# Two feature blocks of each feed-forward in plain form, and its entry's arithmetic on VectorE

## The chip, the cores and the metric

The kernel runs on one core of a Trainium2 chip. A core has five engines with queues of their own: TensorE (PE; its weight loads are PEld), VectorE (DVE), ScalarE (ACT), GpSimd (POOL) and SyncE (SP), which here only starts DMA transfers. An engine works through its queue in order; semaphores make one wait for another. The metric is the time of one execution on the device, in microseconds.

## What is computed

Two decoder layers over 1024 tokens of 1024 features, float32. Layer A mixes by causal attention with a forget gate, layer B by dilated attention in three groups over a shared K/V; each is followed by a norm and a gated feed-forward with a short convolution over the tokens:

```python
def conv_ffn(h, w_up, conv_w, conv_b, w_down):
    u = h @ w_up                        # 1024 -> 2 x 2816
    u = causal_depthwise_conv(u, conv_w, width=3) + conv_b
    a, gate = jnp.split(u, 2, axis=-1)
    return (jax.nn.silu(gate) * a) @ w_down

for layer in (A, B):
    x = x + mixer(rms_norm(x, mix_norm_g)) @ w_out
    x = x + conv_ffn(rms_norm(x, ffn_norm_g), ...)
out = rms_norm(x, final_norm_g)
```

## The kernel before, in words

Activations lie with features on partitions. Every float32 operand of a product is split into a high and a low part (`split`, line 149: ScalarE casts, VectorE subtracts), and a product is three matmuls: high-high, high-low, low-high. The activations that feed a projection are `yh` and `yl`, 8 blocks of 128 features by 1024 tokens. Half the tokens are 512 columns: one matmul, one PSUM bank, and one VectorE instruction of 128x512.

`after_mixer` (line 1053) runs the entry of a feed-forward. `first_half` normalises the first half of the tokens (`norm_half`): sums of squares to TensorE (line 183), the root on small tiles, four transposes (line 196), a copy by ScalarE (line 198); then 8 multiplications, four on VectorE (line 213), four on GpSimd (line 230), whose gains ScalarE has multiplied in beforehand (line 206), and 8 splits. Meanwhile TensorE runs the output projection of the second half (`out_proj`, eight tiles, each added into `xT` by VectorE, line 627). Two PSUM banks serve it, so a tile waits for the addition of the last but one.

The up-projection takes a block of 128 features and its gates at once as a 2 x 2 product in seven products instead of eight (Winograd's form of Strassen's). A are the weights, by halves of the inputs; B the normalised activations: B11 and B21 are the first half of the tokens, B12 and B22 the second. Its operands are sums: S1 to S4 of weights (GpSimd, lines 755 and 757) and T1 to T4 of activations. T1 = B12 - B11, T3 = B22 - B12, T2 = T3 + B11, T4 = B21 - B11 - T3. Only two of seven products per block (A11 B11, A12 B21) need the first half alone. `second_half` normalises the second half and makes T1 to T4, partly on GpSimd (lines 681, 682, 694); B11 and B21 - B11 wait in the tiles of the low parts of T2 and T4, where SP stores them (line 660).

`ffn` lists steps, each with a load, a preparation (sums of weights), a split and a use, issued 6, 5, 3 and 0 steps ahead. The first two feature blocks' steps alternate. Step 1 may only be issued behind the second norm's sums on TensorE, steps 2 and 3 behind its transposes. Weight tiles `wh`, `wl` are rings of six, the raw ones `wraw` of three, `fraw` of two. `tap` (line 713) is the convolution, `middle` the gated value `mh`, `ml`, from which the down-projection (`down_step`) starts as soon as two blocks are there. The final order on every engine is set by the framework's scheduler, which plans with a timeline of its own.

At the exit of layer A's feed-forward `norm_half` runs again for each half, without gains.

Of the kernel before, what the change touches and what calls it, by code (L numbers as in the profile page):

```python
# [50 lines left out]
def trunk(ctx, tc, x, a_w_in, a_b_f, a_w_out, b_w_q, b_w_out, kv_norm_g, w_kv,  # L51
# [25 lines left out]
    # activations that feed the projections: high and low parts, features on partitions  # L77
# [45 lines left out]
    def stream(tasks):  # L123
        """tasks: (load, body); each load is issued one task ahead"""
# [11 lines left out]
    def weave(main, filler, ratio, ready=lambda: True):  # L136
        """ratio columns of filler per column of main, once ready; the filler stops at a None"""
# [30 lines left out]
    def square_sums(fp, xT, hf, ds):  # L168
        """sums over the blocks ds of the squares of half the tokens; also 2 KB of free memory"""
        acc, free = halves(fp.tile([P, S], F32, name="ca" if hf else "cg"))  # L170
# [29 lines left out]

    def gained(y, xT, gain, ds, sl):
        """y = xT * gain, or where that is xT itself"""
        if gain is None:
            return [xT[:, d, sl] for d in ds]
        for i, d in enumerate(ds):
            nc.scalar.activation(y[i], xT[:, d, sl], AF.Identity, scale=gain[:, d:d + 1])
        return y
# [55 lines left out]
    def softmax(t, sc_cuts, masks, nm, l, rl):  # L263
        """t = exp(min(s) - s) / sum, for negated scores s = sc + mask; nm: min(s), l: the sum"""
# [12 lines left out]
    def add_parts(dst, po, tmp, view=lambda t: t):  # L277
        """dst = (value high part) p + (value low part) p, rows 0..63 and 64..127 of po"""
# [68 lines left out]
    def project_v_a(vs, hf, w):  # L347
        """values of two pairs for half the tokens: [token, (block, head, high|low of 64)]"""
# [9 lines left out]
    def scores_a(ap, psc, head, qg):  # L358
        """probabilities of query blocks 2qg, 2qg+1"""
# [56 lines left out]
    # ---------------------------------------------------------------- mixer B  # L416
# [3 lines left out]
    def by_residue(g, hf):  # L420
        """tokens of half hf, residue by residue: views of the source and of the result"""
# [8 lines left out]
    def in_order(g, t, m):  # L430
        """places in token order of columns m*512.. of the residue order"""
# [50 lines left out]
    def scores_b(ap, psc, p, g, j, head, nm, ls, m):  # L482
        """probabilities of half m of the query blocks (in residue order), by (key, query) block"""
# [106 lines left out]
    # ---------------------------------------------------------------- after a mixer  # L590
# [113 lines left out]
    def ffn(l, xT, fp, psu, y3, B, norm):  # L704
# [174 lines left out]
        for i in range(-LOAD, n):  # L879
            if i == 0:  # L880
                first, second = norm()
# [349 lines left out]
```

## Time and profile before

| | before |
|---|---|
| time, median of 3 runs (lowest to highest) | 2719.21 us (2717.98 to 2719.22) |
| span of the profiled execution | 2719.0 us |
| TensorE busy | 2606.2 us (96%), 12937 matmuls |
| VectorE busy | 2049.2 us (75%) |
| ScalarE busy | 1402.8 us (52%) |
| GpSimd busy | 757.3 us (28%) |

The page names no other time for the profiled execution than its span. TensorE's busy time includes matmuls that run into each other, so idle time is read from stretches and from the waits, not from the sum. Layer A's feed-forward has its entry from about 600 to 730 us and its exit at 1325 to 1375, layer B's entry is from about 1970 to 2090.

### The profile page before, as it was taken

Reading aid. Unit: us, or ns where it says so; the run is one execution under the profiler, and the core shown is the slowest. Engines: PE = TensorE matmul, PEld = TensorE weight load, DVE = VectorE, ACT = ScalarE, POOL = GpSimd, SP = SyncE. Lnnn points to the kernel's source line nnn. Section 1 sums busy time; section 2 is a strip of 40 time slices with the busy share of each in tenths; the row PEclk is TensorE's granted clock in tenths of the full one; section 3 lists DMA queues with packets and bytes.
Section 4 is the critical chain, followed back from the end, with each engine's and each line's share of the span. In section 5 each row is a group of like instructions: output and inputs, shape, how many; then the busy total and the mean of one; then the engine's idle time right before and its main releaser. Section 6 shows DMA issues by size and latency. Waiting matters only on the chain. (4 is left out here: it accounts for less than half of the span.)

```text
span 2719.0 us, 38066 instructions
## 1 busy us (share of the span) xinstructions
PE 2606.2 (96%) x12937; PEld 2172.9 (80%) x12937; DVE 2049.2 (75%) x4021; ACT 1402.8 (52%) x2937; POOL 757.3 (28%) x904
## 2 busy tenths in 40 slices
PE   7999999997999999999899999999878999999998
PEld 5899988786788888888688888888657888888887
DVE  5677777768976777778777777777799766777786
ACT  6565665654534344444545566566655443444444
POOL 0222222315212211112243454544353122111121
PEclk8999999999999999999999999999878999999999
DMA  5211211522111111111411111113211111112113
GB/s 178 66 55 51 64 56 59 190 82 83 46 49 54 49 52 54 59 51 46 142 36 37 47 40 40 47 40 100 94 63 47 53 49 54 48 55 59 51 47 113
DMA packets 258619, 176.99 MB, mean 65 GB/s; under 512 B 12528, under 2 KB 240504, under 8 KB 258424
## 3 DMA queue, kind: packets, MB, share of 16 engines
q1 hardware_dynamic: 258424, 174.56, 21.1%
q8 instruction: 102, 1.67, 0.3%
q14 instruction: 93, 0.76, 0.1%
HBM read 146.63 MB, written 23.68 MB: 63 GB/s over the span
## 5 line engine op out<-in xcount | busy, mean ns | idle before, releaser
L114 PE MATMUL mm<-yh,wh 128*128 128x512 f32 (+1 forms) x1008 | 402.7, 400 | 18.3 <-DVE xT L627 6.5
L115 PE MATMUL mm<-yl,wh 128*128 128x512 f32 (+1 forms) x1008 | 401.1, 398 | 0.4 <-DMA yl<-o_sp 0.4
L116 PE MATMUL mm<-yh,wl 128*128 128x512 f32 (+1 forms) x1008 | 400.7, 398 | 0.0
L150 ACT CAST wh<-wraw 128x512 fp32r<-128x512 f32 x230 | 142.1, 619 | 365.6 <-PE up L771 322.4
L771 PE MATMUL up<-yl,wh 128*128 128x512 f32 x704 | 278.3, 396 | 17.7 <-DVE yl L151 17.7
L856 DVE TENSOR_TENSOR xT<-mm,xT 128x512 f32<-128x512 f32 x320 | 217.3, 683 | 101.0 <-PE mm L116 99.5
L151 DVE TENSOR_TENSOR wl<-wraw,wh 128x512 fp32r<-128x512 f32 x230 | 168.3, 736 | 152.3 <-ACT wh L150 152.0
L771 PE MATMUL up<-yh,wh 128*128 128x512 f32 x704 | 276.4, 395 | 6.8 <-ACT yh L150 5.8
L771 PE MATMUL up<-yh,wl 128*128 128x512 f32 x704 | 272.6, 394 | 0.0
L114 PEld LDWEIGHTS mm<-yh,wh 128*128 128x128 f32 (+1 forms) x1008 | 190.0, 189 | 58.2 <-issue 10.6
L115 PE MATMUL mm<-ml,wh 128*128 128x512 f32 x576 | 225.3, 391 | 0.5 <-DVE ml L151 0.5
L116 PE MATMUL mm<-mh,wl 128*128 128x512 f32 x576 | 224.3, 389 | 0.0
L114 PE MATMUL mm<-mh,wh 128*128 128x512 f32 x576 | 224.2, 390 | 0.0
L271 ACT ACTIVATE t<-t,nm 128x128 f32<-128x128 f32 (+4 forms) x320 | 185.2, 580 | 73.0 <-DVE nm L266 69.0
L115 PEld LDWEIGHTS mm<-yl,wh 128*128 128x128 f32 (+1 forms) x1008 | 189.9, 188 | 36.9 <-DVE yl L151 1.0
L116 PEld LDWEIGHTS mm<-yh,wl 128*128 128x128 f32 (+1 forms) x1008 | 189.7, 188 | 37.0 <-issue 0.3
L150 ACT CAST pt<-tp 128x128 fp32r<-128x128 f32 (+2 forms) x408 | 150.2, 382 | 111.1 <-PE tp L244 66.2
L755 POOL TENSOR_TENSOR sraw<-fraw 128x512 f32<-128x512 f32 x42 | 68.2, 1623 | 479.2 <-DMA fraw<-in_ffn_w_up_dram 338.2
L151 DVE TENSOR_TENSOR pt<-tp,pt 128x128 fp32r<-128x128 f32 (+2 forms) x408 | 170.8, 430 | 36.3 <-ACT pt L150 33.5
L257 PE MATMUL po<-pt,v 128*128 128x256 f32 x1040 | 192.8, 292 | 3.4 <-DVE og L280 1.1
L93 DVE TENSOR_TENSOR wl<-wraw,wh 128x512 fp32r<-128x512 f32 (+1 forms) x185 | 138.6, 753 | 60.2 <-ACT wh L92 58.0
L771 PEld LDWEIGHTS up<-yl,wh 128*128 128x128 f32 x704 | 134.1, 190 | 48.5 <-DVE yl L151 20.4
(320 smaller groups left out, 6421.1 us busy)
## 6 DMA issues: line engine op xcount, KB each, us to landing
wraw<-in_ffn_w_down_dram SPq DMA_DIRECT2D x104, 256.0 KB
fraw<-in_ffn_w_up_dram SPq DMA_DIRECT2D x84, 256.0 KB
wraw<-in_ffn_w_up_dram SPq DMA_DIRECT2D x84, 256.0 KB
wraw<-in_a_w_in_dram SPq DMA_DIRECT2D x64, 256.0 KB
wraw<-in_w_kv_dram SPq DMA_DIRECT2D x48, 256.0 KB
wraw<-in_a_w_out_dram SPq DMA_DIRECT2D x32, 256.0 KB
xT<-x_sp SPq DMA_DIRECT2D x32, 256.0 KB
wraw<-in_b_w_q_dram SPq DMA_DIRECT2D x24, 256.0 KB
```

Of the source, the lines that this page charges most:

```text
L93: nc.vector.tensor_tensor(out=wl, in0=raw, in1=wh.bitcast(F32), op=ALU.subtract)
L114: nc.tensor.matmul(ps, ah, bh, start=(i == 0), stop=False)
L115: nc.tensor.matmul(ps, ah, bl, start=False, stop=False)
L116: nc.tensor.matmul(ps, al, bh, start=False, stop=(i == n - 1))
L150: nc.scalar.copy(h, src)
L151: return nc.vector.tensor_tensor(out=l, in0=src, in1=h.bitcast(F32), op=ALU.subtract).ins
L257: nc.tensor.matmul(po[:, col:col + 2 * P], v(kb), pt[:, hl, i * 2 * P:(i + 1) * 2 * P], start=(first and i == 0 and hl == 0), stop=(last a ...
L271: nc.scalar.activation(t[:, :n], t[:, :n], AF.Exp, bias=nm[len(sc_cuts) - 1], scale=-1.0, accum_out=l)
L755: nc.gpsimd.tensor_tensor(out=raw[n], in0=raw[a], in1=raw[b], op=op)
L771: nc.tensor.matmul(ps[bank], a[:, c], b[:, k], start=(start and k == 0 and i == 0), stop=(k == KH - 1 and i == 2), skip_group_check=True)
L856: nc.vector.tensor_tensor(out=xT[:, d, sl], in0=ps, in1=xT[:, d, sl], op=ALU.add)
```

## The change

- Blocks 0 and 1 of both feed-forwards are computed in plain form, with eight products each (`plain`, `PLAIN = 2`). First come all products of both blocks with the first half of the tokens (A11 B11, A12 B21, and the same for the gates' rows A21, A22), then those of the second half, where A B12 is accumulated as A B11 + A T1 in the bank that still holds A B11. Their convolutions and gated values (`rest`) come behind.
- The multiplications of the norms and the sums T1 to T4 are all on VectorE; `gained` (ScalarE's multiplication by gains ahead of GpSimd's) is gone.
- `second_half` is cut in two by a `yield`: first T1 and B22, later T2, T3 and T4. The tiles of T3 hold the weights of block 0 until its last product, that of T2's high part holds the sums of squares.

```diff
     def norm_half(fp, psum, xT, gain, hf, raw):
         sl = half(hf)
-        xg = gained(raw[KH:], xT, gain, range(KH, KD), sl)
         r, _ = feature_rstd(fp, psum, xT, hf)
-        for k in range(KH):
-            normed(raw[k], xT, gain, k, sl, r)
-        for k in range(KH):
-            nc.gpsimd.tensor_tensor(out=raw[KH + k], in0=xg[k], in1=r, op=ALU.mult)
         for d in range(KD):
+            normed(raw[d], xT, gain, d, sl, r)
             split(yh[:, d, sl], yl[:, d, sl], raw[d])
...
     def second_half(fp, psum, y3, xT, gain, B, raw, sums):
...
         for k in range(KH):
             normed(b12[k], xT, gain, k, sl, r)
-        for k in range(KH):
             t1 = half_tile(fp)
             nc.vector.tensor_tensor(out=t1, in0=b12[k], in1=b11[:, k], op=ALU.subtract)
             part("T1", k, t1)
+        for k in range(KH):
+            normed(b22[k], xT, gain, KH + k, sl, r)
+            part("B22", k, b22[k])
+        yield steps
...
         for k in range(KH):
-            with tc.issue_after(done) if k else nullcontext():
-                nc.gpsimd.tensor_tensor(out=b22[k], in0=b22[k], in1=r, op=ALU.mult)
-            done = nc.gpsimd.tensor_tensor(out=t3[k], in0=b22[k], in1=b12[k],
-                                           op=ALU.subtract).ins
-        for k in range(KH):
+            nc.vector.tensor_tensor(out=t3[k], in0=b22[k], in1=b12[k], op=ALU.subtract)
             t2 = half_tile(fp)
             nc.vector.tensor_tensor(out=t2, in0=t3[k], in1=b11[:, k], op=ALU.add)
-            last = part("T2", k, t2)
+            part("T2", k, t2)
...
     def up(f):
...
+            def plain(row, hf):
+                a, b, bank, c = row + "1", row + "2", "X" + row, "ca" if row == "A1" else "cg"
+                if hf:
+                    return [lambda: product(a, "T1", bank, False),
+                            lambda: (product(b, "B22", bank, False), snap(c, 1, bank))]
+                return [lambda: product(a, "B11", bank, True),
+                        lambda: (product(b, "B21", "Q", True), snap(c, 0, "Q"),
+                                 add(c, 0, bank, c, 0))]
...
-        first = [up_steps(f) for f in range(2)]
-        steps = [first[f][i] for i0, i1 in ((0, 2), (2, 3), (3, 4), (4, 5), (5, 6), (6, 7))
-                 for f in range(2) for i in range(i0, i1)]
-        done = 2
+        steps, tails = [], []
+        for f in range(PLAIN):
+            now, then, prep, part, rest = up(f)
+            steps += [(ld, lambda n=n, prep=prep: prep(n), lambda n=n, part=part: part(n), use)
+                      for ld, n, use in now]
+            tails.append((then, rest))
+        for then, _ in tails:
+            steps += [(lambda: None,) * 3 + (use,) for use in then]
+        sums_at = len(steps) - 4
+        rests = {len(steps) - 1 + 3 * f: rest for f, (_, rest) in enumerate(tails)}
```

Over the whole kernel TensorE has 48 matmuls more, VectorE 32 instructions more, ScalarE 28 fewer and GpSimd 64 fewer. TensorE's order is the same outside the entries and a place or two at layer A's exit. Three places show what moved; `mm` are banks of the out-projection and the second norm, `up` those of the up-projection.

TensorE in layer A at the sums of squares of the second half (L183); before, the product ahead of it is A11 B11 of block 0 (`up_7794`):

```order
L771 MATMUL up_7794<-yh_80,wh_7658 128x512
L771 MATMUL up_7794<-yl_81,wh_7658 128x512
L771 MATMUL up_7794<-yh_80,wl_7659 128x512
L183 MATMUL mm_7692<-ones_74,ca_7334 128x1 x4
L771 MATMUL up_7813<-yh_80,wh_7662 128x512
L771 MATMUL up_7813<-yl_81,wh_7662 128x512
```

The same place now, where `mm_7620` is the last tile of the out-projection:

```order
L114 MATMUL mm_7620<-yh_80,wh_7587 128x512
L115 MATMUL mm_7620<-yl_81,wh_7587 128x512
L116 MATMUL mm_7620<-yh_80,wl_7588 128x512
L183 MATMUL mm_7670<-ones_74,T2h_7326 128x1 x4
L765 MATMUL up_7747<-yh_80,T3h_7650 128x512
L765 MATMUL up_7747<-yl_81,T3h_7650 128x512
```

A11 B11 of block 0 now stands one tile earlier, and the sums follow the last tile directly.

VectorE in layer A behind the second norm's root, before; `u` become T1, `sraw` are sums of weights:

```order
L213 SCALAR_TENSOR_TENSOR mh_7252<-xT_6410,gains_988,ca_7334 128x512 x2
L213 SCALAR_TENSOR_TENSOR ml_7253<-xT_6410,gains_988,ca_7334 128x512 x2
L676 TENSOR_TENSOR u_7716<-mh_7252,T2l_7244 128x512
L676 TENSOR_TENSOR u_7720<-mh_7252,T2l_7244 128x512
L676 TENSOR_TENSOR u_7724<-ml_7253,T2l_7244 128x512
L151 TENSOR_TENSOR wl_7852<-sraw_7853,wh_7851 128x512
```

And now, where `mh_7250` and `ml_7251` become B22:

```order
L780 TENSOR_TENSOR ca_7760<-up_7728,ca_7760 128x512
L205 SCALAR_TENSOR_TENSOR mh_7248<-xT_6410,gains_988,T2h_7326 128x512 x2
L205 SCALAR_TENSOR_TENSOR ml_7249<-xT_6410,gains_988,T2h_7326 128x512 x2
L205 SCALAR_TENSOR_TENSOR mh_7250<-xT_6410,gains_988,T2h_7326 128x512 x2
L205 SCALAR_TENSOR_TENSOR ml_7251<-xT_6410,gains_988,T2h_7326 128x512 x2
L673 TENSOR_TENSOR u_7691<-mh_7248,T2l_7243 128x512
L673 TENSOR_TENSOR u_7696<-mh_7248,T2l_7243 128x512
L673 TENSOR_TENSOR u_7701<-ml_7249,T2l_7243 128x512
L673 TENSOR_TENSOR u_7706<-ml_7249,T2l_7243 128x512
L151 TENSOR_TENSOR yl_81<-mh_7250,yh_80 128x512 x2
```

All eight multiplications are on VectorE now and stand together; the splits of weight sums are gone from between them.

TensorE in layer B behind the sums of both halves, before; `up_20473` and `up_20515` are A11 B11 of blocks 0 and 1, `up_20492` is A12 B21 of block 0:

```order
L183 MATMUL up_20083<-ones_74,cg_20084 128x1 x4
L183 MATMUL mm_20371<-ones_74,ca_20157 128x1 x4
L196 MATMUL up_20115<-ident_69,nr_20107 128x128 x4
L196 MATMUL mm_20385<-ident_69,nr_20377 128x128 x4
L771 MATMUL up_20473<-yh_80,wh_20337 128x512
L771 MATMUL up_20492<-yh_80,wh_20341 128x512
L771 MATMUL up_20473<-yl_81,wh_20337 128x512
```

And now, with products of four rows of weights of block 0 and the first two of block 1 (`up_20455`, `up_20468`):

```order
L183 MATMUL up_20051<-ones_74,cg_20052 128x1 x4
L183 MATMUL mm_20325<-ones_74,T2h_20125 128x1 x4
L196 MATMUL up_20083<-ident_69,nr_20075 128x128 x4
L765 MATMUL up_20383<-yh_80,T3h_20305 128x512
L765 MATMUL up_20402<-yh_80,T3h_20305 128x512
L196 MATMUL mm_20339<-ident_69,nr_20331 128x128 x4
L765 MATMUL up_20422<-yh_80,T3h_20305 128x512
L765 MATMUL up_20437<-yh_80,T3h_20305 128x512
L765 MATMUL up_20455<-yh_80,wh_20321 128x512
L765 MATMUL up_20468<-yh_80,wh_20379 128x512
L765 MATMUL up_20383<-yl_81,T3h_20305 128x512
```

Two matmuls moved ahead of the second transposes, and six products of the first half are begun before the first low part (`yl`) is needed.

## Rows read from the trace of the kernel before

**Rows 1.** Stretches: length, then busy us (instructions) of PE PEld DVE ACT POOL, clock, DMA.

```profile
850.00:875.00 25.00, 25.00 (x111) 20.55 (x110) 20.11 (x31) 11.66 (x19) 3.97 (x3) 1.00 0.15 43
655.00:722.00 67.00, 54.49 (x223) 42.30 (x222) 64.85 (x77) 35.09 (x62) 33.55 (x21) 0.92 0.11 32
1345.00:1361.00 16.00, 4.23 (x16) 3.31 (x17) 15.76 (x16) 8.16 (x14) 11.68 (x8) 0.66 0.32 99
1987.00:2080.00 93.00, 68.48 (x248) 51.52 (x247) 87.43 (x100) 47.24 (x82) 52.26 (x32) 0.80 0.16 53
```

**Rows 2.** TensorE's waits, longest in total first: us in total, times, longest.

```profile
PE up L771 <- DVE yl L151: 17.7, 6, 5.9
PE mm L114 <- DVE xT L627: 6.5, 3, 3.5
```

**Rows 3.** Timeline of TensorE, layer A's entry: start us, us, [idle before, what ended it].

```profile
631.65 0.47 PE L114 MATMUL mm<-yh,wh 128*128 128x512 f32 x1 [2.71 <-DVE xT L627]
...
640.84 0.77 PE L114 MATMUL mm<-yh,wh 128*128 128x512 f32 x1 [3.51 <-DVE xT L627]
...
655.89 0.95 PE L183 MATMUL mm<-ones,ca 128*128 128x1 f32 x8
...
674.24 0.79 PE L771 MATMUL up<-yl,wh 128*128 128x512 f32 x1 [5.92 <-DVE yl L151]
...
721.74 0.39 PE L114 MATMUL mm<-mh,wh 128*128 128x512 f32 x1
...
725.31 0.61 PE L771 MATMUL up<-T3h,wh 128*128 128x512 f32 x1 [1.41 <-ACT ca L783]
```

**Rows 4.** Timeline of VectorE, layer A's entry.

```profile
619.82 3.59 DVE L213 SCALAR_TENSOR_TENSOR mh<-xT,gains,cg 128x512 f32<-128x512 f32 x2
...
627.35 1.88 DVE L151 TENSOR_TENSOR yl<-mh,yh 128x512 fp32r<-128x512 f32 x3
629.15 1.75 DVE L151 TENSOR_TENSOR yl<-ml,yh 128x512 fp32r<-128x512 f32 x1
...
661.34 3.61 DVE L213 SCALAR_TENSOR_TENSOR mh<-xT,gains,ca 128x512 f32<-128x512 f32 x2 [0.43 <-ACT ca L198]
```

**Rows 5.** Timeline of GpSimd, layer A's entry.

```profile
619.87 3.00 POOL L230 TENSOR_TENSOR mh<-mh,cg 128x512 f32<-128x512 f32 x2 [18.20 <-ACT cg L198]
...
628.71 1.65 POOL L657 TENSOR_TENSOR mh<-mh 128x512 f32<-128x512 f32 x1 [2.43 <-DVE yl L151]
...
636.21 3.33 POOL L657 TENSOR_TENSOR ml<-ml 128x512 f32<-128x512 f32 x2 [0.63 <-DVE yl L151]
```

**Rows 6.** Timeline of VectorE inside layer A's feed-forward, GpSimd idle.

```profile
859.93 1.41 DVE L721 SCALAR_TENSOR_TENSOR u<-cg,conv,u 128x510 f32<-128x510 f32 x2
```

**Rows 7.** Timeline of TensorE, layer B's entry.

```profile
1987.88 0.95 PE L183 MATMUL up<-ones,cg 128*128 128x1 f32 x8
1990.27 1.05 PE L183 MATMUL mm<-ones,ca 128*128 128x1 f32 x8 [1.44 <-DVE ca L175]
...
2079.34 0.39 PE L114 MATMUL mm<-mh,wh 128*128 128x512 f32 x1
...
2083.78 0.56 PE L771 MATMUL up<-T3h,wh 128*128 128x512 f32 x1 [2.43 <-ACT ca L783]
```

**Rows 8.** Timeline of VectorE, layer B's entry.

```profile
1993.69 3.53 DVE L213 SCALAR_TENSOR_TENSOR mh<-xT,gains,cg 128x512 f32<-128x512 f32 x2 [0.78 <-ACT cg L198]
```

**Rows 9.** A stretch of layer B's out-projection; columns as in rows 1.

```profile
1970.50:1990.30 19.80, 18.04 (x84) 14.70 (x82) 16.74 (x27) 13.25 (x24) 1.30 (x1) 1.00 0.23 67
```

**Rows 10.** Timeline of VectorE, exit of layer A.

```profile
1351.25 5.47 DVE L211 TENSOR_TENSOR T3h<-xT,cg 128x512 f32<-128x512 f32 x4
1356.65 1.75 DVE L175 TENSOR_TENSOR ca<-ca,u 128x512 f32<-128x512 f32 x1
```

**Rows 11.** Timeline of TensorE, exit of layer A.

```profile
1358.45 1.86 PE L183 MATMUL up<-ones,ca 128*128 128x1 f32 x8 [5.03 <-DVE ca L175]
```

More of the change, by code (lines that the diff above doesn't have):

```diff
@@ L631, in out_proj, with side @@
                        for d in range(KD)])
+    PLAIN = 2
+    def side(y3, part):
+        return y3.tile([P, KH, H2], F32R, name=part)
     def sides(y3):
@@ L647, in sides @@
                for n, k, t in (("B11", lo, t0), ("T1", lo, t1), ("B21", hi, t0), ("B22", hi, t1))}
-        for n in ("T2", "T3", "T4"):
-            res[n] = tuple(y3.tile([P, KH, H2], F32R, name=n + p) for p in "hl")
+        for n in ("T2", "T4"):
+            res[n] = (None, side(y3, n + "l"))
         return res
@@ L656, in first_half @@
         for k in range(KH):
-            nc.gpsimd.tensor_tensor(out=raw[KH + k], in0=raw[KH + k], in1=raw[k],
+            nc.vector.tensor_tensor(out=raw[KH + k], in0=raw[KH + k], in1=raw[k],
                                     op=ALU.subtract)
@@ L660, in first_half, with second_half @@
                 nc.sync.dma_start(B[n][1][:, k].bitcast(F32), src)
-    def second_half(fp, psum, xT, gain, B, raw, sums):
+    def second_half(fp, psum, y3, xT, gain, B, raw, sums):
         sl = half(1)
         b11, diff = (B[n][1].bitcast(F32) for n in ("T2", "T4"))
-        b12, b22 = raw[:KH], gained(raw[KH:], xT, gain, range(KH, KD), sl)
+        b12, b22 = raw[:KH], raw[KH:]
         r, steps = feature_rstd(fp, psum, xT, 1, sums)
@@ L677, in second_half @@
             part("T1", k, t1)
+        for k in range(KH):
+            normed(b22[k], xT, gain, KH + k, sl, r)
+            part("B22", k, b22[k])
+        yield steps
+        B["T2"] = (side(y3, "T2h"), B["T2"][1])
+        B["T3"] = (side(y3, "T3h"), side(y3, "T3l"))
+        B["T4"] = (side(y3, "T4h"), B["T4"][1])
         t3 = b12
         for k in range(KH):
-            with tc.issue_after(done) if k else nullcontext():
-                nc.gpsimd.tensor_tensor(out=b22[k], in0=b22[k], in1=r, op=ALU.mult)
-            done = nc.gpsimd.tensor_tensor(out=t3[k], in0=b22[k], in1=b12[k],
-                                           op=ALU.subtract).ins
-        for k in range(KH):
+            nc.vector.tensor_tensor(out=t3[k], in0=b22[k], in1=b12[k], op=ALU.subtract)
             t2 = half_tile(fp)
             nc.vector.tensor_tensor(out=t2, in0=t3[k], in1=b11[:, k], op=ALU.add)
-            last = part("T2", k, t2)
-        with tc.issue_after(last):
-            for k in range(KH):
-                part("T3", k, t3[k])
-        with tc.issue_after(done):
-            for k in range(KH):
-                t4 = half_tile(fp)
-                nc.gpsimd.tensor_tensor(out=t4, in0=diff[:, k], in1=t3[k], op=ALU.subtract)
-                with tc.issue_after(last):
-                    part("T4", k, t4)
-        with tc.issue_after(last):
-            for k in range(KH):
-                part("B22", k, b22[k])
-        return steps
+            part("T2", k, t2)
+        for k in range(KH):
+            part("T3", k, t3[k])
+        for k in range(KH):
+            t4 = half_tile(fp)
+            nc.vector.tensor_tensor(out=t4, in0=diff[:, k], in1=t3[k], op=ALU.subtract)
+            part("T4", k, t4)
+        yield None
     LOAD, PREP, SPLIT = 6, 5, 3
@@ L731, in up @@
             raw, w, t, ps = {}, {}, {}, {}
-            pairs = {}
             def load(*names):
@@ L736, in load @@
                     block, half_ = n[1], int(n[2]) - 1
-                    if f != 1:
-                        raw[n] = (wp.tile([P, H2], F32, name="wraw", bufs=3) if block == "1" else
-                                  fp.tile([P, H2], F32, name="fraw", bufs=2))
-                    else:
-                        if block not in pairs:
-                            pairs[block] = mid_tile(fp, "mh" if block == "1" else "ml")
-                        raw[n] = halves(pairs[block].bitcast(F32))[half_]
+                    raw[n] = (wp.tile([P, H2], F32, name="wraw", bufs=3) if block == "1" else
+                              fp.tile([P, H2], F32, name="fraw", bufs=2))
                     fb = f if block == "1" else NF + f
@@ L748, in prep @@
             def prep(n):
-                w[n] = hl()
+                if f == 0:
+                    if not w:
+                        both = side(y3, "T3h"), side(y3, "T3l")
+                        w.update({m: [t[:, i] for t in both]
+                                  for i, m in enumerate(("A11", "A12", "A21", "A22"))})
+                else:
+                    w[n] = hl()
                 a, b, op = {"S1": ("A21", "A22", ALU.add), "S2": ("S1", "A11", ALU.subtract),
@@ L752, in prep @@
                 if a:
-                    raw[n] = (raw["S1"] if n == "S2" and f < 2 else
-                              fp.tile([P, H2], F32, name="sraw", bufs=2))
+                    raw[n] = fp.tile([P, H2], F32, name="sraw", bufs=2)
                     nc.gpsimd.tensor_tensor(out=raw[n], in0=raw[a], in1=raw[b], op=op)
@@ L806, in c11, with rest @@
                 add("ca", 0, "Q", "cg", 0)
-            none = lambda: None
+            def plain(row, hf):
[6 more added lines that the diff above has]
+                                 add(c, 0, bank, c, 0))]
+            def rest():
+                for hf in range(2):
+                    gate(hf)
+                    middle(hf)
+            none = lambda: None
+            if f < PLAIN:
+                first, second = ([use for row in ("A1", "A2") for use in plain(row, hf)]
+                                 for hf in range(2))
+                return [(lambda n=n: load(n), n, use)
+                        for n, use in zip(("A11", "A12", "A21", "A22"), first)], second, prep, part, rest
             return [
@@ L812, in up @@
                 (lambda: load("A12"), "A12",
-                 lambda: (product("A12", "B21", "Q", True), f != 1 and c11())),
+                 lambda: (product("A12", "B21", "Q", True), c11())),
                 (lambda: load("A21", "A22"), "S1",
-                 lambda: (product("S1", "T1", "Z", True), f == 1 and c11())),
+                 lambda: product("S1", "T1", "Z", True)),
                 (none, "S2",
@@ L880, in ffn @@
             if i == 0:
-                first, second = norm()
+                norm = norm()
+                first, second = next(norm)
+            if i == sums_at:
+                next(norm)
             if 0 <= i + SPLIT < n:
@@ L1068, in after_mixer @@
         first_half(fp, up, xT, g_ffn[l], B, raw)
-        sums = square_sums(fp, xT, 1, blocks_done(out_proj(w_out, 1, xT)))
+        sums = square_sums(fp, xT, 1, blocks_done(out_proj(w_out, 1, xT)),
+                           y3.tile([P, S], F32, name="T2h"))
         for hf in ffn(l, xT, fp, psu, y3, B,
-                      lambda: second_half(fp, mm, xT, g_ffn[l], B, raw, sums)):
+                      lambda: second_half(fp, mm, y3, xT, g_ffn[l], B, raw, sums)):
             yield hf, fp, up if hf else mm, y3
```

13 lines of the change are left out of this document (5 added, 8 removed).

## The prediction

> **What bounds the kernel now.** I read the busy shares of stretches first. Inside a feed-forward TensorE is never idle: 111 matmuls in 25 us, 0.226 us each [rows 1]. At the two entries it is not. From 655 to 722 us it gets through 223 matmuls in 67 us, from 1987 to 2080 through 248 in 93 us, at mean granted clocks of 0.92 and 0.80, so part of that time runs at 1.2 GHz instead of 2.4, and VectorE is busy 65 of 67 and 87 of 93 us [rows 1]. The list of TensorE's waits names the culprit: VectorE's low parts of the normalised activations (17.7 us) and its additions into xT (6.5 us) [rows 2]. So the entries are bound by VectorE, the rest by TensorE's columns. The end of every entry is easy to see on TensorE: the first matmul on `mh`, when the first product of the down projection starts, at 721.74 us in layer A [rows 3] and at 2079.34 us in layer B [rows 7]. I forecast when these two points come now; behind them the order of TensorE is nearly the same again.
>
> Why VectorE is slow there is in its own rows. Two multiplications of the norm take 3.59 us while GpSimd runs two of its own [rows 4, 5]. A little later three splits take 1.88 us with GpSimd silent, and the next one 1.75 us alone, under GpSimd's subtraction at 628.71 [rows 4, 5]. So a VectorE instruction of 128x512 costs 0.60 us of the queue by itself ((1.88 - 0.68)/2; 0.67 for the form with a scalar, from two in 1.41 us [rows 6]) and about 1.7 beside GpSimd. Moving GpSimd's work here takes 0.60 to 0.67 us per step and gives back about 1.1 for each VectorE instruction that was held up.
>
> A rule bears on this. The Trainium skill, "SBUF — State Buffer", section "Who interferes with whom", says that a VectorE instruction with two SBUF inputs and a GpSimd instruction that reads SBUF exclude each other for a whole instruction. The rows show a delay of 1.1 us, less than GpSimd's 1.65 us; by the rule each sum that stays on GpSimd at an entry (about four, for feature block 2) would cost VectorE 1.65 instead of 1.1, some 2 us more per entry, which only matters where VectorE is late (second rival).
>
> **The change, part by part.** *Plain form.* Blocks 0 and 1 take 8 products of 12 matmuls instead of 7: 24 matmuls more per layer, 24 x 0.226 = 5.4 us each time, paid in full once TensorE no longer waits. In exchange 8 products (96 matmuls, 21.7 us) need only the first half of the tokens, where 4 did before, and the other 8 need T1 and B22 only; T2, T3 and T4 are first needed by block 2.
>
> *Layer A, out-projection.* Before, TensorE idles 2.71 and 3.51 us for xT [rows 3], whose additions stand behind the norm in VectorE's queue. That norm starts at 619.82 in both kernels. Now 8 multiplications (8 x 0.67 = 5.4), a weight split and four splits of yl (5 x 0.60 = 3.0) stand ahead of the addition: 628.2, and 0.68 plus hand-over gives 629.0 for TensorE instead of 631.65. The second wait goes: that addition stands 7 instructions (4.2 us) later, while a tile takes TensorE 5.4. Three tiles and the first product (84 matmuls, 19.0 us) end at 648.0. But this product now stands ahead of the last tile, so the sums of squares follow that tile directly and nothing covers addition, square and sum. Layer B shows this gap, from the first sums at 1987.88 to the second at 1990.27: 2.4 us [rows 7]. So the sums run at 650.4 instead of 655.89 [rows 3].
>
> *Layer A, second norm.* Its first multiplication came 5.45 us behind the sums (661.34 [rows 4]); now 655.9. VectorE has one addition, 8 multiplications, 4 differences and 13 others (splits, T3, one addition) up to the last split of T1: 18 x 0.60 + 8 x 0.67 = 16.2, hence 672.1. TensorE meanwhile has 12 + 72 matmuls of the first half and 10 more: 650.4 + 0.9 + 0.4 + 94 x 0.226 = 672.9. So it meets T1 ready, 0.8 us ahead, and runs through: 228 matmuls from sums to `mh`, 51.5 us, so **703.2 instead of 721.74: -18.5 us**, the 24 additional matmuls included. (Before it stops in the middle, for instance 5.92 us until 674.24 [rows 3].) T2 and T4 follow on VectorE in 18 instructions (11 us behind T1), T3's low parts 8 later, while TensorE has 96 matmuls (21.7 us) of plain products to cover them.
>
> *Layer B.* Here both sums come together and no out-projection covers the norm; TensorE waits from 1990 on in any case. The weights of blocks 0 to 2 are now split earlier, 8 splits (4.8 us) more in the out-projection, where VectorE is idle 3.1 of 19.8 us [rows 9]; I take 1.0 us of delay, between 0 and 4.8. The first multiplication moves from 1993.69 [rows 8] to 1994.7. Eight of them and a small step: 2000.3, when TensorE gets past its transposes with four high-part matmuls in hand; the first yl is there at 2001.0. From 2000.5, with 0.4 for transposes and 10 matmuls at half clock (10 x 0.2 = 2.0 us; one shows 0.61 busy there, as against 0.39 [rows 3]), it has 94 matmuls of the first half: 2024.1. VectorE: 46 instructions from 1994.7 (16 x 0.67 + 30 x 0.60 = 28.7) end at 2023.4, again just ahead. Then 144 more: 2024.1 + 32.5 = **2056.6 instead of 2079.34: -22.7 us.**
>
> *Exit of layer A.* Four multiplications take 5.47 us beside GpSimd's, the sum behind them 1.75 [rows 10]; eight alone take 4.8 and the sum ends at 1356.7 instead of 1358.4, so the sums on TensorE (1358.45 [rows 11]) move up by 1.5. The first split is no longer last: **-1.5 us**. The norm of the second half has no waiting TensorE; nothing there.
>
> *What costs nothing.* ScalarE loses 16 multiplications by gains and 12 splits; it was not full. On SP the stores of differences now follow VectorE's, done near 636.5, earlier than GpSimd's (639.5 [rows 5]), so the weight loads behind them are not later. Block 2's S1 gets its weight tile only when block 1's first weight is used up (six tiles in the ring), some 687 us; TensorE needs it at 698. T3's tile holds block 0's weights until its products end, about when VectorE arrives there. Each has 0 to 1 us of stall in it; I take 0.
>
> *Behind `mh`.* Before, TensorE waits once more for ScalarE's copy of a bank, 1.41 and 2.43 us [rows 3, 7], both times with half clock behind. That wait stands in the new order too; I leave it. Its bounds: all of it goes, or VectorE's queue is late there.
>
> Sum: -18.5 - 22.7 - 1.5 = -42.7. The profiled execution spans 2719.0 us and the page gives no other time for it; the median of the three runs is 2719.21, so the span stands for the time: **2676 us.**
>
> **The rivals.** *The wait moves behind the plain products.* From T1 to the last low part of block 1's result VectorE has 55 instructions: at 0.62 us they end at 706.2 and 2057.5, TensorE needs them at 707.5 and 2060.9 (19 matmuls behind `mh`). The slack is only 1.3 and 3.4 us. At the pace of the entries before (65/77 = 0.84 and 87/100 = 0.87 [rows 1]) they take 12.2 and 14.0 us longer, so TensorE waits 10.9 and 10.6: 2698 us. For it: the conv taps, block 2's sums on GpSimd and the weights meet there. Against: GpSimd has four steps there, not twenty.
>
> *VectorE stays slow for reasons of its own; slower than before.* Then its queue is the path throughout: 81 instructions in A for the 51.6 us from 655.9 to 707.5, 101 in B for the 66.2 from 1994.7 to 2060.9. The gains of A's out-projection (5.5) and the exit (1.5) go, which leaves 35.7 to lose; it decides from a mean of (51.6 + 66.2 + 35.7)/182 = 0.84 us. At the exit's pace, 15.76/16 = 0.985 [rows 1], the result is 182 x 0.985 - 153.5 = 26 us slower: 2745. Against it: the splits at 0.60 us in the same stretch [rows 4].
>
> *It also cures the tail.* Both bank waits and nine half-clock matmuls (0.2 each) behind either go: 1.41 + 2.43 + 3.6 = 7.4, thus 2669 us.
>
> That the change does not do what it says is excluded by the order: six products of the first half stand behind the norm's transposes.
>
> **How the numbers follow.** Forecast 0.62, wait behind the products 0.18, tail cured 0.13, slow VectorE 0.04, and 0.03 for mixtures that end near the old time. A measurement of this kernel can tell 0.2% from no change, 5 us. Faster 0.93, same 0.03, slower 0.04. The open terms (B's delay 0 to 4.8, the half clock, small stalls) make the forecast 2668 to 2686; the range must reach into the tail's cure below and the moved wait above: 2660 to 2699 us.
>
> **What would show it.** Right: additions in the out-projection within 1 us; GpSimd silent between first norm and block 2; norm multiplications of 0.67 us; TensorE without a gap from the second transposes to `mh`, some 52 us (A). Wrong: VectorE at over 0.7 us in that stretch; TensorE waiting for T1 or B22; new gaps over 5 us at the first matmuls on `mh`; waits for weights.

## The result and the profile after

The changed kernel takes 2685.69 us (median of four runs, 2681.52 to 2687.63) against 2719.21: ratio 0.987, 95% interval 0.9855 to 0.9884. The forecast was 2676, its range 2660 to 2699. The profiled execution took 2685.47 us, of which the program spans 2683.6; the span is 35.4 us shorter than before, where 42.7 were forecast. TensorE is now busy 2602.9 us (12985 matmuls), VectorE 2004.3, ScalarE 1386.8, GpSimd 655.6.

The stretches that answer to [rows 1] (length, then busy us and instructions of PE, PEld, DVE, ACT, POOL, then TensorE's granted clock, DMA share, GB/s): in layer A TensorE is now busy throughout from 655 us to `mh`; in layer B it has 243 matmuls in 61 us instead of 248 in 93. GpSimd has two instructions in each where it had 21 and 32.

```profile
655.00:709.00 54.00, 54.00 (x232) 44.36 (x233) 47.95 (x79) 30.77 (x53) 3.35 (x2) 0.97 0.06 20
...
1987.00:2048.00 61.00, 58.53 (x243) 47.39 (x244) 59.59 (x94) 34.70 (x59) 3.06 (x2) 0.92 0.15 52
```

TensorE's waits (us in total, times, longest): both leaders of [rows 2] are gone, and a new one heads the list, the sums of squares waiting for VectorE.

```profile
PE mm L183 <- DVE T2h L175: 7.7, 2, 4.2
```

This wait in layer A, on the timelines of TensorE, VectorE and GpSimd (start, us, instruction, idle before and what ended it; columns as in [rows 3]):

```profile
649.17 0.39 PE L116 MATMUL mm<-yh,wl 128*128 128x512 f32 x1
653.10 1.87 PE L183 MATMUL mm<-ones,T2h 128*128 128x1 f32 x8 [3.54 <-DVE T2h L175]
654.83 0.78 PE L765 MATMUL up<-yh,T3h 128*128 128x512 f32 x1
...
709.16 0.39 PE L114 MATMUL mm<-mh,wh 128*128 128x512 f32 x1
...
711.97 0.50 PE L765 MATMUL up<-T3h,wh 128*128 128x512 f32 x1 [1.04 <-ACT ca L777]
```

```profile
651.30 1.75 DVE L175 TENSOR_TENSOR T2h<-T2h,u 128x512 f32<-128x512 f32 x1
...
660.88 1.40 DVE L205 SCALAR_TENSOR_TENSOR mh<-xT,gains,T2h 128x512 f32<-128x512 f32 x2
```

```profile
649.56 1.27 POOL L749 TENSOR_TENSOR sraw<-fraw 128x512 f32<-128x512 f32 x1 [59.65 <-DMA fraw<-in_ffn_w_up_dram]
650.91 1.59 POOL L749 TENSOR_TENSOR sraw<-sraw,wraw 128x512 f32<-128x512 f32 x1
652.58 1.60 POOL L751 TENSOR_TENSOR wraw<-wraw,sraw 128x512 f32<-128x512 f32 x1
```

The out-projection's last matmul starts at 649.17, then TensorE waits 3.54 us; the sums run at 653.10 (before 655.89, [rows 3]). The addition behind the last square (651.30) takes 1.75 us, since GpSimd makes block 2's weight sums at the same moment. The sums then take 1.73 us to the next matmul instead of 0.81 (655.89 to 656.70 before), and the matmuls up to about 658.4 come every 0.43 us. A view of that stretch (columns as in [rows 1]) shows a granted clock of 0.50, that is 1.2 instead of 2.4 GHz:

```profile
653.10:658.40 5.30, 5.30 (x17) 4.53 (x18) 0.83 (x5) 0.21 (x1) 1.08 (x1) 0.50 0.00 0
```

`mh` starts at 709.16 instead of 721.74.

Layer B, TensorE and VectorE: the second sums come 5.18 us behind the first (2.39 before, [rows 7]), again with slow additions; VectorE's first multiplication comes 3.48 us behind the second sums, as before (3.42, [rows 7, 8]). `mh` starts at 2048.42 instead of 2079.34.

```profile
1976.80 1.02 PE L183 MATMUL up<-ones,cg 128*128 128x1 f32 x8 [0.81 <-DVE cg L175]
1981.98 1.87 PE L183 MATMUL mm<-ones,T2h 128*128 128x1 f32 x8 [4.15 <-DVE T2h L175]
...
2048.42 0.39 PE L114 MATMUL mm<-mh,wh 128*128 128x512 f32 x1
```

```profile
1978.51 1.74 DVE L175 TENSOR_TENSOR T2h<-T2h,u 128x512 f32<-128x512 f32 x1
...
1980.36 1.56 DVE L175 TENSOR_TENSOR T2h<-T2h,u 128x512 f32<-128x512 f32 x1
...
1985.46 1.41 DVE L205 SCALAR_TENSOR_TENSOR mh<-xT,gains,cg 128x512 f32<-128x512 f32 x2 [0.57 <-ACT cg L198]
```

Where the time went, in sections of TensorE's timeline, us (start: to the last row of `po` matmuls of layer A's attention; A: to the first matmul on `mh`; tail A: to the first sums at the exit; exit: to its last transposes; attention: to layer B's last row of `po` matmuls; B: to first `mh`; tail B: to the end):

| kernel | start | A | tail A | exit | attention | B | tail B | span |
|---|---|---|---|---|---|---|---|---|
| before | 594.6 | 127.2 | 615.0 | 30.6 | 579.1 | 132.9 | 639.7 | 2719.0 |
| after | 596.0 | 113.2 | 613.5 | 31.1 | 580.4 | 114.2 | 635.1 | 2683.6 |
| e1_vec_only | 591.2 | 115.3 | 617.3 | 29.9 | 578.9 | 125.8 | 640.3 | 2698.8 |
| e2_plain_gp | 594.1 | 121.2 | 611.8 | 30.1 | 580.1 | 124.9 | 635.8 | 2698.0 |
| e3_sums_vec | 596.1 | 110.9 | 612.2 | 30.1 | 579.5 | 108.4 | 636.0 | 2673.2 |
| e4_cover | 596.4 | 107.3 | 613.7 | 30.2 | 577.1 | 111.5 | 636.5 | 2672.5 |
| e5_both | 593.2 | 106.8 | 612.1 | 30.0 | 579.9 | 110.7 | 636.2 | 2668.9 |
| e6_plain1 | 596.1 | 113.4 | 620.3 | 30.3 | 582.7 | 116.8 | 640.6 | 2700.3 |
| e7_exit_gp | 595.8 | 113.7 | 613.6 | 31.2 | 583.7 | 111.8 | 636.4 | 2686.2 |
| e8_load | 593.9 | 113.7 | 616.4 | 30.0 | 582.8 | 114.2 | 637.0 | 2688.0 |

So the change is +1.4 us (start), -14.0 (A), -1.5 (tail A), +0.6 (exit), +1.3 (attention), -18.7 (B), -4.5 (tail B). The start ends between 591.2 and 596.4 us in the ten kernels, though the order up to there is the same in all, on every engine; so spans scatter by some us for reasons ahead of the edits, and the sections tell more than the totals. They scatter too: the attention has the same order on every engine in the changed kernel, e4_cover and e8_load, and takes 580.4, 577.1 and 582.8 us.

### The profile page after: what moved, and what is told of

The parts are those of the page before. It is cut to its first block, busy times and chain, and to the rows that moved or that the text cites. A ratio compares the mean times of both kernels' runs of the same rounds, so it can differ in the third digit from the quotient of the medians.

```text
span 2683.6 us, 38044 instructions
## 1 busy us (share of the span) xinstructions
PE 2602.9 (97%) x12985; PEld 2178.6 (81%) x12985; DVE 2004.3 (75%) x4053; ACT 1386.8 (52%) x2909; POOL 655.6 (24%) x840
## 4 chain that ended last, share of the span: by engine, by line
PE 86%; DVE 7%; ACT 3%; issue 2%; DMA 1%; POOL 1%; POOLq 0%; ACTq 0%; SPq 0%; DVEq 0%
PE up L765 30%; PE mm L114 13%; PE mm L115 13%; PE mm L116 13%; PE po L245 4%; PE tp L232 3%; PE sc L364 1%; PE sc L365 1%; DVE lx L569 1%; DVE u L716 1%; PE up L114 1%; PE sc L487 1%; PE sc L486 1%; PE up L115 1%; PE up L116 1%
## 5 line engine op out<-in xcount | busy, mean ns | idle before, releaser
L870 DVE TENSOR_TENSOR xT<-mm,xT 128x512 f32<-128x512 f32 x320 | 218.2, 685 | 111.5 <-PE mm L116 109.8
L92 ACT CAST wh<-wraw 128x512 fp32r<-128x512 f32 (+1 forms) x185 | 113.6, 618 | 113.5 <-PE mm L115 91.8
```

Source lines behind the costliest of these rows:

```text
L92: nc.scalar.copy(wh, raw)
L870: nc.vector.tensor_tensor(out=xT[:, d, sl], in0=ps, in1=xT[:, d, sl], op=ALU.add)
```

## The experiments

**Each part alone.** e1_vec_only is the kernel before with VectorE's arithmetic and the seven-product form throughout:

```diff
-        for k in range(KH):
-            nc.gpsimd.tensor_tensor(out=raw[KH + k], in0=xg[k], in1=r, op=ALU.mult)
         for d in range(KD):
+            normed(raw[d], xT, gain, d, sl, r)
             split(yh[:, d, sl], yl[:, d, sl], raw[d])
...
```

> The kernel before with only the second part of the change: all multiplications of the norms and T1 to T4 on VectorE, all blocks in seven products. Theory (GpSimd slows VectorE and the seven-product form asks for T1 and T2 too early; each part cures a good half, and the two overlap): sums of squares of layer A near 651 us, TensorE then waits some 4 us each for T1 and for T2, first matmul on mh near 708 to 712 in A and 15 to 20 us earlier than before in B; in all 2690 to 2700 us. Rival 1 (the plain form does all of it): entries as before, 2712 to 2719. Rival 2 (VectorE's speed does all of it and the 48 matmuls of the plain form are a loss): below the changed kernel by up to 10.8 us, 2675 to 2680.

Measured: 2704.76 us, ratio 0.9933 (0.992 to 0.9947). Slower than expected, and neither rival. A is 11.9 us shorter than before, B only 7.1, and the tails lose 2.3 and 0.6. TensorE's timeline:

```profile
664.22 0.80 PE L763 MATMUL up<-yl,wh 128*128 128x512 f32 x1 [3.88 <-DVE yl L151]
...
2002.40 1.12 PE L196 MATMUL mm<-ident,nr 128*128 128x128 f32 x4 [10.16 <-DVE nr L161]
...
2015.64 0.80 PE L763 MATMUL up<-yl,wh 128*128 128x512 f32 x1 [3.59 <-DVE yl L151]
```

The multiplications are quick, but two products per block are too little cover: TensorE waits for T1's low parts in both layers, and in layer B 10.16 us for the second root.

e2_plain_gp is the changed kernel with half of that arithmetic on GpSimd as before:

```diff
-            normed(b22[k], xT, gain, KH + k, sl, r)
+            nc.gpsimd.tensor_tensor(out=b22[k], in0=b22[k], in1=r, op=ALU.mult)
...
-            nc.vector.tensor_tensor(out=t3[k], in0=b22[k], in1=b12[k], op=ALU.subtract)
+            nc.gpsimd.tensor_tensor(out=t3[k], in0=b22[k], in1=b12[k], op=ALU.subtract)
```

> The changed kernel with only the first part: plain form of two blocks, while half of the norms' multiplications (with ScalarE's gains ahead of them), the difference of the first half, T3 and T4 are on GpSimd as before. Theory (as above): VectorE's multiplications take 1.8 us again, the waits for xT in layer A's out-projection (2.7 and 3.5 us) are back, TensorE waits for low parts in layer B; 12 to 20 us slower than the changed kernel: 2695 to 2705. Rival 1 (the plain form covers whatever VectorE needs): within 4 us of the changed kernel, 2682 to 2690. Rival 2 (VectorE's speed is all): near the kernel before plus 10.8 us of matmuls, 2715 to 2730.

Measured: 2700.01 us, ratio 0.9919 (0.9905 to 0.9932), as expected. VectorE's multiplications in layer A, then TensorE's wait there:

```profile
621.37 2.45 DVE L213 SCALAR_TENSOR_TENSOR mh<-xT,gains,cg 128x512 f32<-128x512 f32 x2 [0.39 <-ACT cg L198]
623.74 3.49 DVE L213 SCALAR_TENSOR_TENSOR ml<-xT,gains,cg 128x512 f32<-128x512 f32 x2
```

```profile
639.48 0.50 PE L114 MATMUL mm<-yh,wh 128*128 128x512 f32 x1 [3.63 <-DVE xT L627]
```

Two multiplications take up to 3.49 us again, and the wait for `xT` in layer A is back. In A the parts gain 11.9 (VectorE) and 6.0 us (plain form) alone and 14.0 together. That looks like overlap, but the changed kernel alone has the gap of 3.54 us ahead of the sums (1.1 us in e1_vec_only, 0.61 in e2_plain_gp); with that gap covered (e4_cover, below) both gain 19.9, somewhat more than their sum. In B they gain 7.1 and 8.0 alone and 18.7 together, 3.6 more than their sum, which suggests that each needs the other there: quick operands, and products that don't yet need T1. It is no more than a sign, since B moves by 2.3 to 2.7 us where little but the engines' order differs (e7_exit_gp, e4_cover). Tail B falls by 4.5 us with the plain form (e2_plain_gp: 3.9) and not without (e1_vec_only: +0.6).

**The gap ahead of the sums.** e3_sums_vec moves GpSimd's sums for block 2 to VectorE (`sums_behind` is the last split of B22), e4_cover puts a product into the gap (`last_tile` is the out-projection's last matmul):

```diff
+                eng = nc.vector if f == PLAIN else nc.gpsimd
+                with tc.issue_after(sums_behind[0]) if f == PLAIN else nullcontext():
...
-                    nc.gpsimd.tensor_tensor(out=raw[n], in0=raw[a], in1=raw[b], op=op)
...
+                        eng.tensor_tensor(out=raw[n], in0=raw[a], in1=raw[b], op=op)
...
```

> The changed kernel with block 2's four sums of weights (S1 to S4) on VectorE, queued there behind the last split of B22, none on GpSimd at the entry. Theory (GpSimd's three sums fall into the gap between the last tile of the out-projection and the sums of squares and hold VectorE up by 1.1 us each): the addition into the sum of squares (1.75 us in A, 1.74 and 1.56 in B) takes 0.68; the gap on TensorE goes from 3.7 to about 2.5 us in A and from 5.2 to 2.4 in B, with less half clock behind in A (up to 1.8); 4 to 6 us faster than the changed kernel: 2680 to 2682. Rival (the gap is VectorE's own queue, or four more instructions of 0.6 us on VectorE cost what is won): the gaps stay within 0.5 us, 2685 to 2690.

```diff
             elif i >= 0:
-                steps[i][3]()
+                with tc.issue_after(last_tile) if i == 0 else nullcontext():
+                    steps[i][3]()
...
```

> The changed kernel with the first product (A11 B11 of block 0) tied behind the last tile of the out-projection on TensorE, where it stood before the change. Theory (the last tile is followed by nothing, so the gap of 3.7 us and the half clock behind it, 1.8 us, are paid in full in layer A): sums of squares at about 650.4 instead of 653.1, idle in front of them under 0.5 us, no matmul of 0.43 us behind; first matmul on mh at 704.7 instead of 709.2; layer B as it is; 4.5 us faster than the changed kernel, 2681. Rival (VectorE's second norm sets T1, and TensorE meets it late, or the last tile waits for its weights or its bank): under 1.5 us of it is kept, 2684 to 2686.

Measured: e3_sums_vec 2675.47 us, 0.9828 (0.9815 to 0.9842); e4_cover 2676.29, 0.9834 (0.982 to 0.9847): both about 10 us faster than the changed kernel, more than expected. With e3_sums_vec A falls by 2.3 us; its gap is 2.6 us, and half clock still follows it (0.56 from 652.77 to 656.42 us). B falls by 5.8, but the order on TensorE in B moved too (the first half's transposes stand ahead of the second sums), so not all of it is GpSimd's. With e4_cover A falls by 5.9 us. The 3.3 us less in the attention come with the same order on every engine, so they are scatter; the 2.7 in B come with a shifted order. So of its 10 us some 6 are shown to be the edit's. Its TensorE has no gap at the sums, and the stretch around them has a granted clock of 1.00 (timeline, then stretch):

```profile
649.51 0.39 PE L765 MATMUL up<-yh,T3l 128*128 128x512 f32 x1
649.74 0.95 PE L183 MATMUL mm<-ones,T2h 128*128 128x1 f32 x8
650.55 0.48 PE L765 MATMUL up<-yh,T3h 128*128 128x512 f32 x1
```

```profile
649.70:656.00 6.30, 5.94 (x32) 4.78 (x32) 4.23 (x8) 1.38 (x3) 3.85 (x3) 1.00 0.00 0
```

e5_both has both edits.

> Both edits at once: block 2's sums on VectorE behind the last split of B22, and the first product behind the last tile of the out-projection. Theory (two different losses: the gap in layer A, which the product covers whole, and GpSimd's sums in layer B, which only the move to VectorE cures): layer A as with the product alone (first mh at 703 to 704.5), layer B's stretch from the first sums to mh as with the moved sums (69.8 us, against 71.6 in the changed kernel) with the transposes of the first half ahead of the second sums; 14 to 16 us faster than the changed kernel, 2668 to 2671. Rival (both cure the same loss, since each alone gave about 10 us): 2674 to 2677.

Measured: 2672.44 us, ratio 0.9821 (0.9806 to 0.9835), the fastest here, a little above the theory's 2668 to 2671 and below the rival's 2674 to 2677. The intervals of e3_sums_vec, e4_cover and e5_both lie wholly below the changed kernel's (0.9855 to 0.9884); among the three the totals can't be told apart, so neither theory of e5_both is decided by the total. A takes 106.8 us, 6.4 below the changed kernel. Layer B, TensorE and the two last additions on VectorE:

```profile
1965.27 1.02 PE L183 MATMUL up<-ones,cg 128*128 128x1 f32 x8 [0.88 <-DVE cg L175]
1967.78 1.87 PE L183 MATMUL mm<-ones,T2h 128*128 128x1 f32 x8 [1.48 <-DVE T2h L175]
```

```profile
1966.24 0.68 DVE L175 TENSOR_TENSOR T2h<-T2h,u 128x512 f32<-128x512 f32 x1
...
1967.03 0.69 DVE L175 TENSOR_TENSOR T2h<-T2h,u 128x512 f32<-128x512 f32 x1
```

With GpSimd silent the additions take 0.69 us instead of 1.74 and 1.56, and the second sums follow the first by 2.51 us instead of 5.18. That is near the 2.4 us which the prediction had read from [rows 7]. But B as a whole is only 0.8 us shorter than in e4_cover, where the sums are 4.93 us apart.

**One plain block** (`PLAIN = 1`, a size).

> The changed kernel with one feature block in plain form instead of two (24 matmuls less over the two layers, 5.4 us). Theory (two blocks are what covers VectorE's way to T1, T2 and T4): TensorE has 60 matmuls behind the sums of layer A instead of 94 before it needs T1, and T2 is needed 8 products later instead of 16; it waits some 6 to 8 us for T1 and more for T2 in both layers: 5 to 11 us slower than the changed kernel, 2691 to 2697. Rival (VectorE alone at full speed is quick enough, the second block is a pure loss): 5 us faster, 2680.

Measured: 2701.80 us, ratio 0.9929 (0.9914 to 0.9944): slower than either theory said, by 16 us against the changed kernel. A is level, though 24 matmuls fewer (5.4 us) stand in it: 12 are saved, and 12 now stand behind `mh`. TensorE waits 1.24 us for T1 there, and 3.7 for weights and a bank's copy. B, with 24 fewer as well, takes 2.7 us longer. The tails lose 6.8 and 5.4, of which the 12 matmuls are 2.7 each:

```profile
671.39 0.50 PE L765 MATMUL up<-yl,T3h 128*128 128x512 f32 x1 [1.24 <-DVE yl L151]
...
725.17 0.50 PE L765 MATMUL up<-yh,wl 128*128 128x512 f32 x1 [2.06 <-DVE wl L151]
...
736.89 0.50 PE L114 MATMUL mm<-mh,wh 128*128 128x512 f32 x1 [1.83 <-DVE xT L870]
```

So the second block covers not only the way to T1 but a backlog of VectorE and ScalarE, which shows at weights and a bank's copy ahead of `mh` and, 15 to 30 us behind it, at weights' low parts and `xT`. I had looked at T1 and T2 alone.

**The exit.** e7_exit_gp puts four multiplications of the exit's norms back on GpSimd:

```diff
-            normed(raw[d], xT, gain, d, sl, r)
+            if gain is None and d >= KH:
+                nc.gpsimd.tensor_tensor(out=raw[d], in0=xT[:, d, sl], in1=r, op=ALU.mult)
+            else:
+                normed(raw[d], xT, gain, d, sl, r)
```

> The changed kernel with four of the eight multiplications of the norms at layer A's exit back on GpSimd, as before. From the first sums on TensorE there to the last transposes the kernel before takes 30.6 us, the changed one 31.1, where 1.5 less was forecast. Theory (VectorE's eight multiplications are slowed by GpSimd's multiplications of layer B's weights by gains, 8.0 us instead of 4.8, so the split hardly matters): 30.5 to 31.5 us, total within 1 us of the changed kernel apart from layer B's attention, 2684 to 2688. Rival (the exit did gain 1.5 us and something else at the exit lost it): 32 to 33 us, 2687 to 2689.

Measured: 2684.23 us, ratio 0.9864 (0.9849 to 0.9879), not to be told from the changed kernel, and within the theory's range. The exit on TensorE, e7_exit_gp:

```profile
1323.06 0.95 PE L183 MATMUL mm<-ones,cg 128*128 128x1 f32 x8
...
1342.93 1.87 PE L183 MATMUL up<-ones,ca 128*128 128x1 f32 x8 [3.96 <-DVE ca L175]
...
1354.22 0.60 PE L196 MATMUL up<-ident,nr 128*128 128x128 f32 x4
```

The same in the changed kernel:

```profile
1322.70 0.95 PE L183 MATMUL mm<-ones,cg 128*128 128x1 f32 x8
...
1344.12 1.87 PE L183 MATMUL up<-ones,ca 128*128 128x1 f32 x8 [5.75 <-DVE ca L175]
...
1353.84 0.60 PE L196 MATMUL up<-ident,nr 128*128 128x128 f32 x4
```

The second sums come 19.87 us behind the first with GpSimd's help and 21.42 without (21.70 before, to 1358.45 in [rows 11]), the transposes 31.16 and 31.14 (30.58 before). So sums that come 1.6 us earlier don't bring the transposes forward. What stands between them is half clock: from the sums to the transposes the granted clock is 0.58 over 11.29 us in e7_exit_gp (with one wait of 0.40 us in them), 0.62 over 9.72 in the changed kernel and 0.70 over 8.88 before, for the same matmuls. VectorE and GpSimd of the changed kernel say why its sums weren't quicker:

```profile
1335.34 5.02 DVE L203 TENSOR_TENSOR T3h<-xT,cg 128x512 f32<-128x512 f32 x4
1340.29 3.08 DVE L203 TENSOR_TENSOR T3l<-xT,cg 128x512 f32<-128x512 f32 x4
```

```profile
1334.89 1.43 POOL L89 TENSOR_TENSOR wraw<-wraw,gains 128x512 f32<-128x512 f32 x1 [3.27 <-DVE xT L870]
1336.49 1.28 POOL L89 TENSOR_TENSOR wraw<-wraw,gains 128x512 f32<-128x512 f32 x1 [0.17 <-DMA wraw<-in_w_kv_dram]
1338.43 1.39 POOL L89 TENSOR_TENSOR wraw<-wraw,gains 128x512 f32<-128x512 f32 x1 [0.66 <-DVE T3h L203]
```

The eight multiplications take 8.0 us, not the 4.8 forecast from [rows 10]: three of GpSimd's multiplications of layer B's weights by gains fall into them. (B is 2.3 us shorter in e7_exit_gp, where no line of it was edited; the order on TensorE differs there.)

**The price of GpSimd beside VectorE**, by itself. e8_load adds four multiplications on GpSimd behind the second norm's root; nothing uses them:

```diff
+        junk = side(y3, "T4h").bitcast(F32)
+        for k in range(KH):
+            nc.gpsimd.tensor_tensor(out=junk[:, k], in0=xT[:, k, sl], in1=r, op=ALU.mult)
```

> The changed kernel with four additional multiplications of 128x512 on GpSimd in either layer, behind the root of the second norm, into memory that is free there; nothing uses them. Theory (each GpSimd instruction holds VectorE up by 1.1 us, and TensorE meets T1 just when it is ready): VectorE's eight multiplications take 5.3 + 4 x 1.1 = 9.7 us, TensorE waits 2 to 4.4 us for T1 in each layer and runs the next matmuls at half clock; 6 to 10 us slower than the changed kernel, 2692 to 2696. Rival 1 (they exclude each other for GpSimd's whole instruction, 1.65 us): 5.3 + 6.6 = 11.9 us, 10 to 14 us slower, 2696 to 2700. Rival 2 (TensorE has a reserve there): within 2 us, 2684 to 2688.

Measured: 2690.09 us, ratio 0.9888 (0.9871 to 0.9904): some 4 us slower, between the theory and its second rival; the intervals of the two kernels overlap, so the rows decide. Layer A, VectorE (eight multiplications, the last row T1's first low part) and GpSimd, then TensorE's first matmul on that low part and its wait behind `mh`:

```profile
659.27 3.46 DVE L205 SCALAR_TENSOR_TENSOR mh<-xT,gains,T2h 128x512 f32<-128x512 f32 x2
662.66 3.49 DVE L205 SCALAR_TENSOR_TENSOR ml<-xT,gains,T2h 128x512 f32<-128x512 f32 x2
...
675.35 0.68 DVE L151 TENSOR_TENSOR yl<-u,yh 128x512 fp32r<-128x512 f32 x1
```

```profile
659.19 6.41 POOL L669 TENSOR_TENSOR T4h<-xT,T2h 128x512 f32<-128x512 f32 x4 [7.16 <-ACT T2h L198]
```

```profile
676.98 0.39 PE L769 MATMUL up<-yl,T3h 128*128 128x512 f32 x1
...
712.66 0.79 PE L769 MATMUL up<-T3h,wh 128*128 128x512 f32 x1 [2.18 <-ACT ca L781]
```

The same low part and its matmul in the changed kernel:

```profile
672.79 0.69 DVE L151 TENSOR_TENSOR yl<-u,yh 128x512 fp32r<-128x512 f32 x1
```

```profile
678.58 0.39 PE L765 MATMUL up<-yl,T3h 128*128 128x512 f32 x1
```

The eight multiplications take 9.46 us (659.27 to 668.73) instead of 5.29: 1.04 for each GpSimd instruction. The low part is there at 676.03 and used at 676.98; without the load at 673.48 and 678.58. So TensorE had 5.1 us of reserve at T1, and no wait appears there. (The prediction's 0.8 us set T1's last split against TensorE's first matmul on T1; TensorE takes the low parts later than that, one by one.) Layer A loses 2.9 us behind `mh`, where the wait for the bank's copy is 2.18 instead of 1.04 us and a granted clock of 0.71 follows until 718 us, against 1.00 in the changed kernel (tail A 616.4).

## Why the prediction was nearly right

- **What bounds the kernel** was right: with both parts TensorE runs through to `mh` from the second sums in A and from the second transposes in B, and each part alone gives half of the change or a little more (e1_vec_only, e2_plain_gp).
- **VectorE's prices** were right: 1.40 us for two multiplications, 0.62 us for an instruction on average from 640 to 703 us (50.69 us, 82 instructions). About 1.1 for one held up was measured as 1.04. The rule of the Trainium skill ("SBUF — State Buffer", "Who interferes with whom"), exclusion for a whole instruction, I had priced with GpSimd's 1.65 us. That was a misreading of a row: such a duration contains GpSimd's own wait for VectorE. In e8_load two of each take 3.46 us, which is 2 x (0.67 + 1.04): the two engines take turns, as far as durations can show it. But a GpSimd instruction with two full operands, as in e8_load, takes 1.29 us where VectorE is idle (the changed kernel, below), so VectorE loses some 0.25 us less than that; exclusion for the whole of the duration in the rows is not shown.

```profile
1226.29 1.29 POOL L749 TENSOR_TENSOR sraw<-fraw 128x512 f32<-128x512 f32 x1 [9.84 <-DVE xT L870]
```

- **Layer A** was mis-sized: -14.0 instead of -18.5. The prediction saw that the first product had left the gap ahead of the sums and priced it with layer B's 2.4 us. It did not ask what else runs there, and put the half clock behind the gap at nothing. GpSimd's three sums for block 2, which the prediction set near `mh` (its first rival), run from 649.56 us on and made it 3.9 us from matmul to sums, against 2.6 in e3_sums_vec (VectorE's addition 1.75 instead of 0.68). TensorE fell to its lower clock, in e3_sums_vec as well, so that is the gap's and not GpSimd's alone; and the first multiplication came 7.8 us behind the sums instead of 5.45. Of the 4.5 us, 1.3 lie ahead of the sums (57.1 us after the `po` matmuls instead of 55.8) and 3.3 between them and `mh` (56.1 instead of 52.8). With the gap filled the section is 19.9 us (e4_cover) and 20.4 us (e5_both) shorter than before, near 18.5 and the 2.4 of the gap together.
- **Layer B**: -18.7 instead of -22.7, in part the same step. Measured from the last `po` matmuls, the first multiplication comes 3.95 us later than before, where the step had 1.0; 2.8 of it is the longer gap between the sums. In e5_both it comes 2.0 us later and the section is 22.2 us shorter than before. Either shift is within the step's bounds of 0 to 4.8. What the gap alone is worth there stays open: e4_cover keeps a gap of 4.93 us, and its B is still 2.7 us shorter than the changed kernel's, with both halves' transposes ahead of the products.
- **Exit**: +0.6 instead of -1.5. The step read four multiplications beside GpSimd's four as 5.47 us and assumed that GpSimd would then be silent; it had the weights of the next layer to multiply. It also took the transposes to follow the sums, which e7_exit_gp refutes: half clock between them takes up what earlier sums give.
- **Tail**: -6.0 in all, taken as nothing. The rival "it also cures the tail" came true in layer B, where wait and half clock are gone, and for a part in A (the wait goes from 1.41 to 1.04 us; the half clock behind it is gone, 1.00 from 711.9 to 716.0 us against 0.58 from 725.3 to 729.4 before). It is the plain form that does this. TensorE's order differs from before for some 90 us behind `mh`, though, more than was said ahead of the result, and what that adds is not separated.
- The rival of a wait behind the plain products did not come, but e6_plain1 shows some of it with one block: 6.8 us in the two tails, without the 12 matmuls that moved into either. The rival of a VectorE that stays slow fell with its mean of 0.62 us.

Of the 7.3 us between forecast and measurement, A is 4.5, B 4.0, exit 2.1, start 1.4, attention 1.3 and the tails -6.0. The misses were larger than their sum: that the forecast came this near owes something to the tails, which it had at nothing, and start and attention are scatter.

## What to carry to other kernels

When an edit takes work out of a gap between two dependent steps, list every engine's instructions that may drift into it, those that nobody waits for among them; here three sums on GpSimd made gaps of 2.6 and 2.5 us into 3.9 and 5.2. Where two engines get in each other's way, the duration of a disturbed instruction contains its own wait: price the disturbance by what the other engine loses, and find out with dummy work how much reserve the waiting engine has. With four GpSimd multiplications added VectorE's delay showed not at T1, the operand that looked critical, but behind `mh`. Fix order by a dependency where a cover matters, since the scheduler moved the covering product ahead of the last tile.

## What the runs showed beside

- A short idle time can cost more than itself: 3.5 us of waiting in layer A took some 2 us more, until the granted clock rose from 0.50 again (56.1 us from sums to `mh` against 53.9 in e4_cover). It need not, as the next point shows.
- With the same order on every engine the start took 591.2 to 596.4 us. 4.1 of these 5.2 us arise in its first 126 us. There TensorE waits 2.9 us for VectorE near 72 us in all ten kernels, and what follows differs: in e1_vec_only and e4_cover, the shortest and the longest start, the next 6 us (columns as in [rows 1]) have a granted clock of 1.00 and of 0.50, with 28 and 14 matmuls. From 60 to 85 us it is 1.00 in three kernels, 0.93 in four and 0.86 in three. Why the same wait is followed by either stays open.

```profile
71.42:77.42 6.00, 6.00 (x28) 5.01 (x29) 3.14 (x6) 2.33 (x5) 1.16 (x3) 1.00 0.37 77
72.62:78.62 6.00, 6.00 (x14) 4.76 (x15) 2.72 (x6) 1.85 (x4) 1.15 (x3) 0.50 0.27 55
```

- An edit in one place moved the scheduler's order in another: B changed by 2.3 us in e7_exit_gp. A difference of 2 or 3 us between two such kernels can't be put down to the edit without its own rows.
